# First loads side by side, and the first weights' high part in halves, in a hybrid retention and attention layer

## The chip, the cores and the metric

The kernel runs on one core of one Trainium2 chip. The metric is the device time of one execution in microseconds (us), of which the median over several runs is taken. A core has TensorE (PE in the profile; PEld are its weight loads, which overlap its matmuls), VectorE (DVE), ScalarE (ACT), GpSimd (POOL) and SyncE (SP), which here only issues DMAs. ACT can issue DMAs too, on a queue of its own.

## The reference

One decoder layer on x of 1 x 2048 x 1024 in float32. The input is normalised, one projection makes all parts, two groups of heads run side by side, and a projection back is added to x.

```python
h = rms_norm(x, norm_w)
proj = einsum('bsd,de->bse', h, w_in)          # 1024 -> 2816
rq, rk, rv, rg, sq, sk, sv, sg = split(proj)
ro = retention(rotary(rq), rotary(rk), rv)     # 4 heads, chunks of 128, decaying state
ro = group_norm(ro) * ret_norm_w * silu(rg)
so = sliding_window_attention(sq, sk, sv, ...) # 8 heads, window 128, sinks, bias
so = so * silu(sg)
x = x + einsum('bse,ed->bsd', concat([ro, so]), w_out)
```

## The kernel before

**Products.** The two projections are four big products over the 2048 rows (2048 x 1024 by columns of `w_in` from 768, from 0 and from 1792, then by `w_out`). Each is done with seven block products instead of eight (a Strassen scheme), for pairs of 128-row chunks. `weights` (L528) makes the seven combinations of a weight's four quarters, `blocks` (L583) those of x. Each operand is held as a high part in the matmul's reduced format (fp32r) and a low part that holds the rest; a block product is, for each of four blocks k of 128 rows of the weights, three matmuls: high x by high w, high x by low w, low x by high w (`passes` in `products`, L662). `split` (L479) makes the two parts: ACT copies the raw tile to the high part, scaled by a column of norm_w (`nw_sb`) where it is a raw weight, and DVE makes raw minus high.

**The opening.** The first four products of the first projection run together. `opening` (L630) loads, for each of four blocks k, the columns of x that they need (`xfirst[k]`, 128 x 512) and splits them in two halves of 256 columns; `products` runs for k < 3 all four high by high matmuls, then all four by the low w, then all four with the low x, so that the parts are needed one after the other (L692 to L698). The very first product matmul needs the first half of the high x of k = 0 and the high w of k = 0.

**Ahead of it.** The last part of `layer` (from L1370) loads `nw_sb` from ACT's queue (cost `BESIDE`, L411), makes a zero tile `none`, runs WARM matmuls on it (`warm`, L1376 to L1380; each shows as two in the profile) and one ACT instruction (`once`) that brings in ACT's table.

**The order of work.** Every instruction is an operation with a cost per engine, the tiles that it reads and writes, and a due time. `Program.emit` (L158) is a planner that runs when the kernel is built: it keeps a clock for every engine and for the DMA queue (Q, which is SP), and always takes the operation that can start first, the one due sooner where they tie; this gives the order in which each engine gets its instructions. An operation with several engines in its cost goes to the one that can start it first. `load` (L413) goes to Q unless a cost is given. All operations pass through one helper, so that nearly every instruction has line L362 in the profile, and tiles tell them apart: `acc` are the banks of the products, `w` and `x` the operands' tiles, `m` the other matmuls' banks.

Of the kernel before, what the change touches and what calls it, by code (L numbers as in the profile page):

```python
# [30 lines left out]
F32R = mybir.dt.float32r  # L31
I32 = mybir.dt.int32
AF = mybir.ActivationFunctionType
ALU = mybir.AluOpType
# [3 lines left out]
S, D = 2048, 1024  # L38
P = 128
NCH = S // P  # L40
NP = NCH // 2
KT = D // P
# [37 lines left out]
OPENING = 4  # L80
SEM = 0.06

WARM = 4

BACKLOG = 1.5

# [37 lines left out]
class Program:  # L124
# [5 lines left out]
    def op(self, cost, go, r=(), w=(), due=0.0, table=None, label="", also=()):  # L130

        o = Op()
        o.cost, o.go, o.due, o.after, o.set, o.label = cost, go, due, [], table, label
        o.n, o.left, o.ready, o.end, o.seen, o.by = len(self.ops), 0, 0.0, 0.0, 0.0, None
        deps = set()
        for b in r:
            if b.writer is not None:
                deps.add(b.writer)
        for b in w:
            if b.writer is not None:  # L140
                deps.add(b.writer)
            deps.update(b.readers)
        for b in r:
            b.readers.append(o)
        for b in w:
            b.writer, b.readers = o, []
        o.bufs = list(dict.fromkeys((*r, *w, *also)))
        for b in o.bufs:
            b.left += 1
        o.new = [b for b in (*w, *also) if b.ap is None and b.tag]  # L150
        for d in deps:
            if d is not o:
                d.after.append(o)
                o.left += 1
        self.ops.append(o)
        return o
# [142 lines left out]
def dve(n, two=False, lat=0.08):  # L299
    return (0.067 + n / 960, 0.067 + n / 960 + lat, two)  # L300


def act(n, more=0.0):
    return (0.094 + n / 1200 + more, 0.2 + n / 1200 + more, False)
# [6 lines left out]
def both(n):  # L311
    return {"V": dve(n, True)}
# [21 lines left out]
def dma(kb, issue=0.45):  # L334
    return {"Q": (0.45 + kb / 1024, 2.6, issue)}
# [27 lines left out]


@with_exitstack
def layer(ctx, tc, xt, xfirst, xtok, nw, w_in, w_rn, qkw, sinks, biasg, rope, dmask, gpow, w_out, out):
    nc = tc.nc
    order = Order(tc)
    V, G, A, Q, T = (Engine(order, e) for e in (nc.vector, nc.gpsimd, nc.scalar, nc.sync, nc.tensor))
# [16 lines left out]
    op = prog.op  # L386

    def kb(name, share, dtype=F32):
        return Buf("k", None, dtype, name, share)
# [10 lines left out]
    def fixed(shape, name, dtype=F32):  # L400
        return Buf(name=name, ap=const.tile(shape, dtype, name=name))
# [5 lines left out]
    def given(ap):  # L407
        return Buf(ap=ap)


    BESIDE = {"A": (0.4, 3.5, False)}  # L411

    def load(b, src, due, kbytes=256, to=lambda t: t, cost=None, also=(), of=lambda t: t):  # L413
        op(
            cost or dma(kbytes), lambda e: e.dma_start(to(b()), of(src())), [src], [b], due, label=f"load {b.name}",
            also=also,
        )
# [4 lines left out]
    def f(t):  # L422
        return t.bitcast(F32)

    ident = fixed([P, P], "ident")
    nw_sb = fixed([P, KT], "nw_sb")
    wr = fixed([P, 4], "wr")
    gp = fixed([P, 2], "gp")
    snk = fixed([P, AH], "snk")
# [98 lines left out]
    def weights(src, c0, n, scale, base, seq):  # L528


        W = {m: [None] * 4 for m in range(1, 8)}
        at = {m: base + seq.first[m] for m in W}
        col, cols = scale

        def raw(q, i, due):
            t = kb("w", "wr")
            k, c = 4 * (q // 2) + i, c0 + q % 2 * n
            load(
                t, given(src[k * P : (k + 1) * P, c : c + n]), due - 3, n // 2, lambda t: t[:, :n],
            )  # L540
            return t

        def by(k):
            return (col, k) if k < cols else None

        def part(m, i, t, scale=None):
            W[m][i] = split(t, n, at[m] - 1.5 + 0.1 * i, "wh", "w", scale)

        b11, b21, t1, t2 = ([None] * 4 for _ in range(4))
        for i in range(4):  # L550
            due = at[1] - 2 + 0.1 * i
            t = b11[i] = raw(0, i, due)
            part(1, i, t, by(i))
        for i in range(4):
            b21[i] = raw(2, i, at[2] - (2 if base else 0.9) + 0.1 * i)
            part(2, i, b21[i], by(4 + i))
        for i in range(4):
            t = b11[i]
            op(
                {"A": act(n, 0.09), "V": (0.13 + n / 1920, 0.2 + n / 1920, True)},  # L560
                lambda e, t=t, i=i: e.activation(t()[:, :n], t()[:, :n], AF.Copy, scale=col()[:, i : i + 1])
                if e is A
                else e.tensor_scalar(t()[:, :n], t()[:, :n], col()[:, i : i + 1], None, op0=ALU.mult),
                [t, col, W[1 if base else 2][3][1]], [t], at[1] + 2 + i, label="scale w",
            )
        for i in range(4):
            due = at[6] - 6 + 0.5 * i
            b12, b22 = raw(1, i, due), raw(3, i, due)
            t1[i] = combine(b12, b11[i], ALU.subtract, n, due, b12, scale=by(i))
            t2[i] = combine(b22, t1[i], ALU.subtract, n, due, b22, scale=by(4 + i))  # L570
            part(6, i, t2[i])
        for i in range(4):
            part(5, i, t1[i])
        for i in range(4):
            due = at[7] - 4 + 0.5 * i
            part(7, i, combine(t2[i], b11[i], ALU.subtract, n, due, b11[i]))
            part(4, i, combine(b21[i], t2[i], ALU.subtract, n, due, b21[i], scale=by(4 + i)))
        for i in range(4):
            part(3, i, raw(3, i, at[3] - 2 + 0.1 * i), by(4 + i))
        return W  # L580
# [49 lines left out]
    def opening():  # L630

        made = []
        for k in range(KT // 2):
            t, hi, lo = kb("x", "raw"), kb("x", "x", F32R), kb("x", "x", F32R)

            load(t, given(xfirst[k]), -4.95 + 0.1 * k)
            parts = []
            for i in range(2):
                c, due = slice(i * 256, (i + 1) * 256), -2.0 + 0.1 * k + 0.01 * i
                h, l = (Part(t, lambda t, c=c: t[:, c]) for t in (hi, lo))  # L640
                op(
                    {"A": act(256), "V": dve(256)} if k == 0 else {"A": act(256)},
                    lambda e, t=t, h=h, c=c: e.activation(h(), t()[:, c], AF.Copy) if e is A else e.tensor_copy(h(), t()[:, c]),
                    [t], [h], due, label="hi x", also=(hi, lo),
                )
                op(
                    both(256), lambda e, t=t, h=h, l=l, c=c: e.tensor_tensor(l(), t()[:, c], f(h()), ALU.subtract),
                    [t, h], [l], due, label="lo x", also=(hi, lo),
                )
                parts.append((h, l))  # L650
            made.append((hi, lo, parts))
        return made
# [4 lines left out]
    def products(B, W, n, base, seq, sink, plus=None, opening=None):  # L657


        s, u, t, bank = {}, {}, {}, {}  # L660

        def passes(m, acc, xh, xl, cols, k, d, goes_on, parts, which):  # L662


            wh, wl = W[m][k]

            def go(e):
                for i in which:
                    a, b = ((xh, wh), (xh, wl), (xl, wh))[i]
                    e.matmul(  # L670
                        acc()[:, :n], a()[:, cols], b()[:, :n], start=(not goes_on and k == i == 0),
                        stop=(k == 3 and i == 2), skip_group_check=goes_on,
                    )

            pairs = ((parts[0], wh), (parts[0], wl), (parts[1], wh))
            reads = list(dict.fromkeys(b for i in which for b in pairs[i]))
            op(f32r(n, len(which)), go, reads, [acc, turn], d, label=f"product {m}", also=(xh, xl, wh, wl))

        for m, p in seq.all:
# [12 lines left out]
            elif p == OPENING - 1:  # L692
                for k, (xh, xl, parts) in enumerate(opening):

                    for which in ((0,), (1,), (2,)) if k < 3 else ((0, 1, 2),):
                        for q in range(OPENING):
                            due = (OPENING * k + q) / 4
# [670 lines left out]


    make_identity(nc, ident())  # L1370
    load(nw_sb, given(nw), -9, 4, cost=BESIDE)

    pw, none = ps(), kb("none", "att")
    op({"V": (0.2, 0.3, False)}, lambda e: e.memset(none()[:, 0:256], 0.0), [], [none], -9, label="nothing")
# [1 line left out]
    def go(e):  # L1376
        for _ in range(WARM):
            e.matmul(pw()[:, 0:256], none()[:, 0:P], none()[:, 0:256], start=True, stop=True)

    op({"T": (0.85 * WARM, 0.85 * WARM + 0.2, False)}, go, [none], [pw], -9, label="warm")  # L1380

# [5 lines left out]
        label="no values",  # L1387
# [34 lines left out]


_SHAPES = {
    "xt": (NCH, P, KT * P), "xfirst": (KT // 2, P, OPENING * P), "xtok": (NCH, P, D), "nw": (P, KT), "w_in": (D, 2816), "w_rn": (P, 4),
    "qkw": (P, 2, HD), "sinks": (P, AH), "biasg": (P, 2, GRP, 320), "rope": (NCH, P, 2, 256),
    "dmask": (P, RH, P), "gpow": (P, 2), "w_out": (D, D),
}
# [89 lines left out]
```

## Time and profile before

| | |
|---|---|
| median of three runs | 717.34 us (717.23 to 718.02) |
| the profiled execution | 717.6 us |
| its span, first to last instruction | 715.3 us |
| PE busy | 710.6 us (99%) |
| DVE, ACT busy | 603.5 us (84%), 437.1 us (61%) |
| first product's weight load | 4.71 us |
| HBM read, written | 110.44 MB, 42.01 MB |

The times inside the span are counted from its first instruction. A row of a view names the engine, the operation, the tiles (written <- read), the shapes and the number of instructions; the bracket at the end tells how long the engine was idle before and what ended that. A row with a q behind the engine's name is an issue of a DMA, and its duration is that of the issue, not of the transfer. Matmul records are pipelined: one lasts longer than the step to the next.

### The profile page before, as it was taken

What the parts mean: (1) busy time and instruction counts of PE and PEld (TensorE: products, weight loads), DVE (VectorE), ACT (ScalarE), POOL (GpSimd) and SP (SyncE); (2) the same over time, 40 slices, a digit from 0 to 9 for tenths busy, and PEclk for the clock granted to TensorE, in tenths of its full rate; (3) what the DMA queues carried; (4) which work ended last, traced back from release to release, by engine and by line L of the source; (5) the groups of instructions that cost most, each with busy time, mean ns of one, the idle gap of its engine ahead of it and who ended that gap; (6) DMA issues with size and microseconds to landing.
All of it is one profiled execution on the core that took longest, in us unless ns stands there. A gap on an engine that the chain in (4) does not pass through costs nothing.

```text
span 715.3 us, 15310 instructions
## 1 busy us (share of the span) xinstructions
PE 710.6 (99%) x5388; PEld 608.9 (85%) x5388; DVE 603.5 (84%) x1456; ACT 437.1 (61%) x1071; POOL 43.6 (6%) x75
## 2 busy tenths in 40 slices
PE   9999999999999999999999999999999999999998
PEld 7888888889999999988888888888888888888886
DVE  6999877876999777899899899878999998677762
ACT  8565966657776465787687875686875437321500
POOL 1000000025111000001000001000000000000000
PEclk9999999999999999999999999999999999999999
DMA  9978948966657268979896585199391422223722
GB/s 329 360 250 309 399 133 305 306 233 219 223 160 222 75 204 255 331 240 320 278 318 192 148 282 159 47 360 371 112 325 52 148 88 75 89 88 119 264 97 95
DMA packets 102028, 153.46 MB, mean 215 GB/s; under 512 B 11840, under 2 KB 40512, under 8 KB 101952
## 3 DMA queue, kind: packets, MB, share of 16 engines
q1 hardware_dynamic: 101808, 152.49, 63.5%
q8 instruction: 42, 0.69, 0.4%
q14 instruction: 34, 0.28, 0.1%
q10 hardware_dynamic: 144, 0.00, 0.0%
HBM read 110.44 MB, written 42.01 MB: 213 GB/s over the span
## 4 chain that ended last, share of the span: by engine, by line
PE 99%; DVE 0%; issue 0%
PE acc L362 81%; PE m L362 18%; DVE t L362 0%; DVE none L362 0%
## 5 line engine op out<-in xcount | busy, mean ns | idle before, releaser
L362 PE MATMUL acc<-w,x 128*128 128x512 f32 (+1 forms) x2700 | 604.4, 379 | 0.0
L362 PEld LDWEIGHTS acc<-w,x 128*128 128x128 f32 x2700 | 489.0, 188 | 79.6 <-issue 4.3
L362 DVE TENSOR_TENSOR x<-x 128x512 fp32r<-128x512 f32 (+2 forms) x220 | 145.1, 680 | 17.7 <-ACT x L362 16.5
L362 ACT ACTIVATE x<-x 128x512 fp32r<-128x512 f32 (+1 forms) x187 | 111.4, 617 | 13.6 <-PE acc L362 10.0
L362 ACT ACTIVATE pm<-lg,nm 128x128 f32<-128x128 f32 x128 | 49.8, 391 | 29.3 <-DVE lg L362 28.0
L362 DVE TENSOR_TENSOR w<-w 128x512 fp32r<-128x512 f32 (+3 forms) x96 | 61.6, 666 | 6.2 <-ACT w L362 6.0
L362 DVE TENSOR_TENSOR s<-acc,s 128x512 f32<-128x512 f32 (+1 forms) x64 | 41.8, 654 | 21.3 <-PE acc L362 20.9
L362 ACT ACTIVATE w<-w 128x512 fp32r<-128x512 f32 (+1 forms) x72 | 40.5, 600 | 26.4 <-DMA w<-in_w_out 18.4
L362 DVE SCALAR_TENSOR_TENSOR w<-w,nw_sb 128x512 fp32r<-128x512 f32 (+3 forms) x72 | 49.9, 709 | 0.7 <-ACT w L362 0.7
L362 DVE CUSTOM_DVE_ANT_0 lg<-m,bias,nsnk 128x160 f32<-128x160 f32 x128 | 42.5, 378 | 4.5 <-PE m L362 4.3
L362 POOL TENSOR_SCALAR_AFFINE_SELECT own<-pT 64x512 f32<-64x512 f32 x32 | 27.4, 868 | 257.3 <-ACT pT L362 227.0
L362 ACT ACTIVATE x<-go 128x512 fp32r<-128x512 f32 x40 | 23.8, 623 | 24.2 <-PE acc L362 21.0
L362 DVE TENSOR_TENSOR t<-acc,t 128x512 f32<-128x512 f32 (+2 forms) x33 | 21.0, 636 | 16.4 <-PE acc L362 16.2
L362 ACT ACTIVATE s<-acc 128x512 f32<-128x512 f32 (+1 forms) x32 | 17.9, 567 | 26.0 <-PE acc L362 20.1
L362 DVE TENSOR_TENSOR t<-acc,s 128x512 f32<-128x512 f32 (+1 forms) x32 | 21.0, 655 | 10.9 <-PE acc L362 10.7
L362 ACT ACTIVATE w<-w,nw_sb 128x512 fp32r<-128x512 f32 (+3 forms) x43 | 27.9, 682 | 3.0 <-DMA w<-in_w_in 1.9
L362 DVE TENSOR_TENSOR r<-acc,t 128x512 f32<-128x512 f32 (+1 forms) x32 | 20.9, 653 | 8.6 <-PE acc L362 7.7
L362 DVE TENSOR_TENSOR x<-go,x 128x512 fp32r<-128x512 f32 x40 | 27.1, 681 | 0.0
L362 ACT ACTIVATE ro<-ro,nmu,rg 128x128 f32<-128x128 f32 x64 | 25.1, 483 | 0.1
L362 ACT ACTIVATION_READ_ACCUMULATOR pm<-lg,nm 128x1 f32 x128 | 24.1, 189 | 0.0
L362 ACT ACTIVATE xk<-xk 128x512 f32<-128x512 f32 x32 | 19.8, 619 | 6.3 <-DMA xk<-in_xtok 6.3
L362 ACT ACTIVATE pT<-m 128x512 f32<-128x512 f32 x32 | 18.6, 595 | 5.9 <-PE m L362 5.6
(132 smaller groups left out, 695.4 us busy)
## 6 DMA issues: line engine op xcount, KB each, us to landing
x<-in_xt SPq DMA_DIRECT2D x80, 256.0 KB, 5.1
x<-s_dram SPq DMA_DIRECT2D x64, 256.0 KB, 4.1
w<-in_w_in SPq DMA_DIRECT2D x40, 256.0 KB, 5.4
s_dram<-x SPq DMA_DIRECT2D x32, 256.0 KB, 4.9
xk<-in_xtok SPq DMA_DIRECT2D x32, 256.0 KB, 5.1
res<-in_xtok SPq DMA_DIRECT2D x32, 256.0 KB, 3.2
w<-in_w_out SPq DMA_DIRECT2D x20, 256.0 KB, 4.5
aq<-aq_dram SPq DMA_DIRECT2D x16, 256.0 KB, 4.4
```

Source lines behind the costliest of these rows:

```text
L362: return lambda *a, **k: self.order.put(op(*a, **k))
```

## The change

The scale of the rows, norm_w, no longer has a load of its own. On the host it is put beside the first block of `xfirst` in one array (`xnw`, 128 x 520); one load from SP brings both into a fixed tile `x_nw`, of which `first_x` and `nw_sb` are parts. The load of the first raw weight tile goes to ACT's queue instead. The high part of that weight is made in two halves of 256 columns, the first on ACT, the second on DVE (`first_split`); the low part comes as before in one DVE instruction. Of the first x, the first half's high part is fixed to DVE and the second's to ACT, with other due times. WARM goes from 4 to 3. A product that reads high w of k = 0 now names both halves.

```diff
-WARM = 4
+WARM = 3
...
-    BESIDE = {"A": (0.4, 3.5, False)}
+    BESIDE = {"A": (0.4, 3.3, False)}
...
-    nw_sb = fixed([P, KT], "nw_sb")
+    x_nw = fixed([P, OPENING * P + KT], "x_nw")
+    first_x = Part(x_nw, lambda t: t[:, : OPENING * P])
+    nw_sb = Part(x_nw, lambda t: t[:, OPENING * P :])
...
+        def first_split(raw, n, due):
+            hi, lo = kb("w", "wh", F32R), kb("w", "wh", F32R)
+            parts = [Part(hi, lambda t, i=i: t[:, i * n // 2 : (i + 1) * n // 2]) for i in range(2)]
+            for i, part in enumerate(parts):
+                def go(e, i=i, part=part):
+                    src = raw()[:, i * n // 2 : (i + 1) * n // 2]
+                    if i == 0:
+                        e.activation(part(), src, AF.Copy, scale=col()[:, 0:1])
+                    else:
+                        e.tensor_scalar(part(), src, col()[:, 0:1], None, op0=ALU.mult)
+                cost = {"A": act(n // 2, 0.09)} if i == 0 else {"V": (0.13 + n / 1920, 0.2 + n / 1920, True)}
+                op(cost, go, [raw, col], [part], due, label="hi w", also=(hi, lo))
+            op(
+                {"V": (0.13 + n / 960, 0.21 + n / 960, True)},
+                lambda e: e.scalar_tensor_tensor(
+                    lo()[:, :n], raw()[:, :n], col()[:, 0:1], f(hi()[:, :n]), op0=ALU.mult, op1=ALU.subtract
+                ),
+                [raw, *parts, col], [lo], due - 2, label="lo w", also=(hi,),
+            )
+            return hi, lo, parts
...
                 t, given(src[k * P : (k + 1) * P, c : c + n]), due - 3, n // 2, lambda t: t[:, :n],
+                BESIDE if base == q == i == 0 else None,
...
-            part(1, i, t, by(i))
+            if base == i == 0:
+                W[1][0] = first_split(t, n, due + 0.5)
+            else:
+                part(1, i, t, by(i))
...
-            t, hi, lo = kb("x", "raw"), kb("x", "x", F32R), kb("x", "x", F32R)
-            load(t, given(xfirst[k]), -4.95 + 0.1 * k)
+            t = kb("x", "raw") if k else first_x
+            hi, lo = kb("x", "x", F32R), kb("x", "x", F32R)
+            if k:
+                load(t, given(xfirst[k - 1]), -4.95 + 0.1 * k)
...
+                if k == 0:
+                    due -= 1.0
...
-                    {"A": act(256), "V": dve(256)} if k == 0 else {"A": act(256)},
+                    ({"V": dve(256)}, {"A": act(256)})[i] if k == 0 else {"A": act(256)},
...
-                    [t], [h], due, label="hi x", also=(hi, lo),
+                    [t], [h], due + (1.6 if k == 0 and i else 0), label="hi x", also=(hi, lo),
...
-            wh, wl = W[m][k]
+            wh, wl, *halves = W[m][k]
+            whole = halves[0] if halves else (wh,)
...
-            pairs = ((parts[0], wh), (parts[0], wl), (parts[1], wh))
+            pairs = ((parts[0], *whole), (parts[0], wl), (parts[1], *whole))
...
-    load(nw_sb, given(nw), -9, 4, cost=BESIDE)
+    op(dma(258), lambda e: e.dma_start(x_nw(), xnw), [], [first_x, nw_sb], -9, label="load x")
```

More of the change, by code (lines that the diff above doesn't have):

```diff
@@ L365, in layer @@
 @with_exitstack
-def layer(ctx, tc, xt, xfirst, xtok, nw, w_in, w_rn, qkw, sinks, biasg, rope, dmask, gpow, w_out, out):
+def layer(ctx, tc, xt, xfirst, xtok, xnw, w_in, w_rn, qkw, sinks, biasg, rope, dmask, gpow, w_out, out):
     nc = tc.nc
@@ L1424 @@
 _SHAPES = {
-    "xt": (NCH, P, KT * P), "xfirst": (KT // 2, P, OPENING * P), "xtok": (NCH, P, D), "nw": (P, KT), "w_in": (D, 2816), "w_rn": (P, 4),
+    "xt": (NCH, P, KT * P), "xfirst": (KT // 2 - 1, P, OPENING * P), "xtok": (NCH, P, D), "xnw": (P, OPENING * P + KT), "w_in": (D, 2816), "w_rn": (P, 4),
     "qkw": (P, 2, HD), "sinks": (P, AH), "biasg": (P, 2, GRP, 320), "rope": (NCH, P, 2, 256),
@@ L1490 @@
     x2 = x.reshape(NCH, P, KT, P)
+    first = x2[: 2 * OPENING : 2, :, : KT // 2].transpose(2, 3, 0, 1).reshape(KT // 2, P, OPENING * P)
     given = {
         "xt": x2.transpose(0, 3, 2, 1).reshape(NCH, P, KT * P),
-        "xfirst": x2[: 2 * OPENING : 2, :, : KT // 2].transpose(2, 3, 0, 1).reshape(KT // 2, P, OPENING * P),
+        "xfirst": first[1:],
         "xtok": x.reshape(NCH, P, D),
-        "nw": norm_w.reshape(KT, P).T,
+        "xnw": np.concatenate([first[0], norm_w.reshape(KT, P).T], axis=1),
         "w_in": w_in[:, _columns()],
```

## The prediction

> **What bounds the kernel now.** I read the first and fourth parts of the page, then three stretches of the span, then the chain's first pieces.
>
> ```profile
> PE 710.6 (99%) x5388; PEld 608.9 (85%) x5388; DVE 603.5 (84%) x1456; ACT 437.1 (61%) x1071; POOL 43.6 (6%) x75
> ...
> PE 99%; DVE 0%; issue 0%
> ```
>
> ```profile
> 5.00:155.00 150.00, 150.00 (x666) 124.18 (x665) 129.28 (x238) 102.26 (x230) 5.29 (x16) 1.00 0.85 295
> 155.00:563.00 408.00, 408.00 (x4050) 358.29 (x4049) 362.03 (x1039) 288.89 (x760) 35.42 (x48) 1.00 0.68 223
> ```
>
> ```profile
> 1.26 3.78 PE m L362 x8
> 5.04 149.67 PE acc L362 x660
> ```
>
> PE is busy for the whole of both stretches (second and third figures of each row equal) and for 710.6 of 715.3 us in all. The 4.7 us without PE work are the 1.26 before the warming matmuls and the end (3.4), which the change does not touch. So no product waits for anything once the products run; a product matmul comes every 149.67/660 = 0.227 us. Time can be won or lost in three ways only: by when the first product starts, by the rate of the first products, and by the order that the planner writes for the rest. The first of these is to be read in the timeline of the opening, in order of time per engine, with the time from issue to landing of the first transfers (last column of the five lines of the second fence, each from the stretch of its own issue: w, nw, x, the second w, the second x).
>
> ```profile
> 0.81 0.41 ACTq L362 DMA_DIRECT2D nw_sb<-in_nw  x1
> ...
> 0.81 0.39 SPq L362 DMA_DIRECT2D w<-in_w_in  x1
> ...
> 1.25 0.42 SPq L362 DMA_DIRECT2D x<-in_xfirst  x1
> ...
> 1.73 0.42 SPq L362 DMA_DIRECT2D w<-in_w_in  x1
> ...
> 3.87 0.72 ACT L362 ACTIVATE w<-w,nw_sb 128x512 fp32r<-128x512 f32 x1 [1.12 <-DMA nw_sb<-in_nw]
> ...
> 4.30 0.29 DVE L362 CAST x<-x 128x256 fp32r<-128x256 f32 x1 [3.10 <-DMA x<-in_xfirst]
> 4.49 0.40 ACT L362 ACTIVATE x<-x 128x256 fp32r<-128x256 f32 x1
> ...
> 4.62 0.75 DVE L362 SCALAR_TENSOR_TENSOR w<-w,nw_sb 128x512 fp32r<-128x512 f32 x1
> 4.71 11.30 PEld L362 LDWEIGHTS acc<-w,x 128*128 128x128 f32 x50 [0.40 <-ACT w L362]
> ...
> 5.29 0.76 DVE L362 TENSOR_TENSOR x<-x 128x256 fp32r<-128x256 f32 x2
> 5.96 0.72 ACT L362 ACTIVATE w<-w,nw_sb 128x512 fp32r<-128x512 f32 x1 [1.07 <-DMA w<-in_w_in]
> 6.64 0.73 ACT L362 ACTIVATE x<-x 128x256 fp32r<-128x256 f32 x2
> ```
>
> ```profile
> w<-in_w_in SPq DMA_DIRECT2D x1, 256.0 KB, 2.8
> nw_sb<-in_nw ACTq DMA_DIRECT2D x1, 4.0 KB, 3.0
> x<-in_xfirst SPq DMA_DIRECT2D x1, 256.0 KB, 3.0
> w<-in_w_in SPq DMA_DIRECT2D x1, 256.0 KB, 4.2
> x<-in_xfirst SPq DMA_DIRECT2D x1, 256.0 KB, 4.4
> ```
>
> The first w is there at 0.81 + 2.8 = 3.6, the row scales nw at 3.8, the first x at 1.25 + 3.0 = 4.3. ACT makes the high part of w from 3.87 to 4.59; DVE makes the first half of the high x from 4.30 to 4.59. Two chains end together, and PE's first weight load starts 0.12 later, at 4.71.
>
> **The change part by part.**
>
> **Loads.** The load of nw goes; its 4 KB travel as eight columns more of the first x (258 KB in place of 256). That load becomes SP's first, at 0.81 instead of 1.25; the first w goes to ACT's queue at 0.81, in nw's place, so ACT's own work (table load, `once`) does not move. SP's later loads each go out one place, about 0.48 us, sooner (the second w at 1.25 in place of 1.73). Side by side in this way is not in the trace, so it is bounded. At best each lands 2.8 after its issue, as the first w did: both at 3.6. At worst, as the same 512 KB move through the same DMA engines, the later of the two lands when the second did before: 4.3. Nw, which ran beside w on the other queue, took 3.0 with its 4 KB, more than w with 256 KB, so the queues do share the engines; I take the middle, T = 3.95, and keep 3.6 to 4.3.
>
> [...]
>
> **High parts.** Before, w's high part was ready to be made when x was still on its way; now neither half can start before T, since nw comes with x. DVE does the high x first (an earlier due time, both ready at once), then the second half of the high w. The price of that half (256 columns, scaled) is not in the trace; the nearest rows are the CAST above (0.29) and DVE's scaling of 512 columns:
>
> ```profile
> L362 DVE TENSOR_SCALAR w<-w,nw_sb x3: 476/476/478, 14.0 to 15.4; 128x512 f32<-128x512 f32 x3
> ```
>
> Bounds 0.24 (half of it) and 0.48; I take 0.31, near the CAST. ACT's half, with 0.40 for 256 columns of x and (0.72 in the rows above for 512 scaled) at most 0.5, ends before DVE's pair. First product: T + 0.02 (landing to CAST, as 4.28 to 4.30) + 0.29 + 0.02 + 0.31 + 0.12 = T + 0.76. For T = 3.6 / 3.95 / 4.3 that is 4.36 / 4.71 / 5.06, against 4.71 now: 0.35 earlier, nothing, 0.35 later. The earlier x and the longer work behind it pay for each other.
>
> **Behind it, on DVE and ACT.** By the planner's rule (earliest start first) DVE's order becomes high x, high w half, low x half, low w, low x half. The high half ends 0.12 before the first product starts (the hop to PE); then come a low half (0.34: half of the step from 5.29 to the pair's end at 6.05, less their overlap) and the low w (0.75), and the hop again: ready 0.34 + 0.75 = 1.1 after the first product's start. It is needed after four matmuls, 4 x 0.227 = 0.9 at full rate and 1.1 with the first at the slow rate of the fences below: its cover (now 5.37 + 0.12 = 5.5, needed at 5.8) is gone, and 0 to 0.2 us of wait follow; I take 0.05. The second half of the high x moves on ACT from 4.49 to about T + 0.5 = 4.45 and is needed two matmuls in: hidden. The second block of rows starts after twelve matmuls, near 4.71 + 12 x 0.227 + 0.2 = 7.6; its high x is ready at 6.64 + 0.42, so 0.4 to 0.5 us of cover remain even if the first product is 0.35 earlier and the loads land no sooner. So no stall follows there; if the loads do land sooner, the cover only grows. No wait is added that has other work queued behind it on ACT: before T it has only the table load and `once`.
>
> **Warming.** One warming matmul of four goes. How it is paid is seen in PE's own groups (duration minimum/median/maximum; the warming weight loads and matmuls, then product matmuls before 5.2, then from 5.4):
>
> ```profile
> L362 PEld LDWEIGHTS m<-none x8: 287/337/337, 1.3 to 4.0; 128*128 128x128 f32 x8
> L362 PE MATMUL m<-none x8: 634/634/794, 1.3 to 4.4; 128*128 128x256 f32 x8
> ```
>
> ```profile
> L362 PE MATMUL acc<-w,x x2: 390/468/546, 4.7 to 5.1; 128*128 128x512 f32 x2
> ```
>
> ```profile
> L362 PE MATMUL acc<-w,x x38: 387/389/397, 5.4 to 13.8; 128*128 128x512 f32 x38
> L362 PEld LDWEIGHTS acc<-w,x x37: 187/188/188, 5.6 to 13.8; 128*128 128x128 f32 x37
> ```
>
> A weight load takes 337 ns in the warming and 188 in the products, the first product matmul 546 and all later ones 389: PE's clock rises to full at about 4.9 us, 3.6 us after PE's first work at 1.26, in the midst of the first product. The page's granted clock reads 1.00 throughout and does not show that step. The eight warming instructions (two for each matmul) start every (4.4 - 1.3)/7 = 0.44 us, so six have passed by 1.26 + 6 x 0.44 = 3.9 in place of 4.8 for eight. The matmul that goes therefore reached to where products start now; kept, it would hold up a product that came sooner. Between 3.9 and 4.7 PE would now stand idle for 0.8 us. My choice: the clock still rises near 4.9, as over three quarters of the time before it are busy. Then an earlier start counts only half (matmuls before 4.9 run at half rate), a later one fully.
>
> **The planner.** Its own clock sees the first product about 0.3 us sooner and the loads one place sooner, and the order of the rest can shift. Every order that keeps PE fed gives the same sum of matmuls; what differs is how often PE changes between products and the small matmuls. The nearest row is the weight loader's idle time at such changes:
>
> ```profile
> PEld m L362 <- issue: 9.1, 44, 0.4
> ```
>
> About 0.2 us each; I cost the new order at nothing, with bounds of three changes fewer or more, -0.6 and +0.6.
>
> **Sum.** Against the profiled execution, 717.6 with 2.3 around its span of 715.3: start 0 (-0.2 to +0.35), low w +0.05 (0 to +0.2), order 0 (-0.6 to +0.6): 717.6 + 0.05. That run lies 0.26 above the median of the three, 717.34, so the forecast is 717.4, its own range 716.6 to 718.3.
>
> **The rivals.**
>
> **The clock rises later (slower).** With one warming matmul fewer the work before 4.7 is 2.6 us and then there is a hole of 0.8. If the rise needs unbroken work of the length seen now (1.26 to 4.9, 3.6 us), the count starts again at the first product and the rise comes at 4.71 + 3.6 = 8.3. All product matmuls from 4.71 to 8.3 then run at half rate; now it is only those to 4.9. Cost (3.6 - 0.2)/2 = 1.7 us: 719.1, 0.24% slower. It decides from the point where 2.6 us of work and a pause of 0.8 are too little for the rise. For it: the rise comes so soon after the fourth warming matmul's end. Against: nothing shows that a shorter stretch or one with a hole would not do. Chance 0.28.
>
> [...]
>
> **The planner's order (either way).** From 7 of the 44 changes, 1.4 us, it crosses the line: 715.9 or 718.8, or a transfer placed late leaves PE waiting, which nothing does now. For it: DVE at 129 of 150 us and DMA at 0.85 in the first stretch leave little room there. Against: PE is never short in 707 us, and a uniform shift changes no comparison in the planner. Slower 0.08, faster 0.12, the latter because the forecast has no other road to a large gain.
>
> **Side by side works at its best.** Both land at 3.6, products from 4.36: half of 0.35, 0.2 us gained, 717.2. It lies inside the forecast. **The change does nothing:** both interleave fully (T = 4.3) and the start comes 0.35 later: 717.7, inside it too.
>
> **How the numbers follow.** A measurement of this kernel can tell about 0.2%, 1.4 us, from no change. Forecast with the two cases inside it 0.52 (within), clock 0.28 and order 0.08 (slower), order 0.12 (faster). Faster 0.12, same 0.52, slower 0.36. For 8 in 10 the range reaches over the clock's 719.1 plus 0.2, and below to 716.4, where most of the faster order is left out: 716.4 to 719.3.
>
> **What would show it.** Right: the first product between 4.4 and 5.1; the two first loads landing between 3.6 and 4.3; on DVE the CAST, then a 256-column scaling of about 0.3; product matmuls of 389 ns from about 4.9 on; PE full between 5 and 563. The clock rival: product matmuls well above 389 ns to about 8.3. The order rival: PE idle, or more or fewer changes, behind 155. Wrong outright: a first product before 4.3, or a PE wait at the second block of rows near 7.6.

## The result, and the profile after

The changed kernel takes 719.62 us (median of 22 runs, 717.49 to 720.29), the kernel before 717.38 (22 runs, 716.93 to 718.53). The ratio of the runs is 1.0023, with a 95% interval of 1.0016 to 1.0031: slower, by an interval that leaves out no change. (It is the ratio of the means, 719.26 and 717.59, and not that of the two medians, 1.0031: the changed kernel's runs form two groups, six from 717.49 to 717.88 and sixteen from 719.24 to 720.29 with nothing between, and the median lies in the upper one.) The median, 719.62, lies 0.3 above the range predicted (716.4 to 719.3); by the ratio the change makes 719.0 of the 717.34 that the forecast started from, which lies inside. Either way it is outside the likeliest case's own range: it is the rival of the late clock that came true, with another loss added that I had bounded too low.

The time around the span, from 1.7 to 3.0 us in all these runs, differs from run to run, so spans are compared from here on. Before (its spans in the runs beside the experiments): 715.1 to 716.7, median 715.8 in 32 runs and 715.9 in 35 others. Changed: six from 715.8 to 716.1, sixteen from 717.5 to 718.5.

The profile of the change happens to be of the lower group (717.88, span 716.1). Its page, engines' busy time and chain:

```profile
PE 710.0 (99%) x5386; PEld 608.5 (85%) x5386; DVE 603.7 (84%) x1456; ACT 437.4 (61%) x1072; POOL 42.2 (6%) x75
...
PE 99%; DMA 1%; ACT 0%; DVE 0%; issue 0%; ACTq 0%
```

PE's busy time is the same within 0.6. A DMA has come into the chain, which before was PE alone from the warming on (all but DVE's zero tile ahead of it). The chain's first pieces in order of time (start, duration) show which:

```profile
0.81 4.29 DMA w<-in_w_in
5.74 150.62 PE acc L362 x663
```

The first w, now on ACT's queue, takes 4.29 us to land, and products start at 5.74, where they started at 4.7. The transfers issued first, with their time to landing in the last column:

```profile
x_nw<-in_xnw SPq DMA_DIRECT2D x1, 260.0 KB, 4.1
w<-in_w_in ACTq DMA_DIRECT2D x1, 256.0 KB, 4.3
```

Before, x took 3.0 and w 2.8. The timeline of the opening, from the first warming matmul on:

```profile
1.26 2.93 PE L362 MATMUL m<-none 128*128 128x256 f32 x6 [1.26 <-DVE none L362]
...
4.93 0.30 DVE L362 CAST x<-x_nw 128x256 fp32r<-128x256 f32 x1 [3.73 <-DMA x_nw<-in_xnw]
5.14 0.35 DVE L362 TENSOR_SCALAR w<-w,x_nw 128x256 fp32r<-128x256 f32 x1
5.18 0.51 ACT L362 ACTIVATE w<-w,x_nw 128x256 fp32r<-128x256 f32 x1 [2.44 <-DMA w<-in_w_in]
...
5.74 0.75 DVE L362 SCALAR_TENSOR_TENSOR w<-w,x_nw 128x512 fp32r<-128x512 f32 x1
5.74 10.34 PEld L362 LDWEIGHTS acc<-w,x 128*128 128x128 f32 x46 [2.28 <-ACT w L362]
5.74 10.54 PE L362 MATMUL acc<-w,x 128*128 128x512 f32 x45 [1.56 <-ACT w L362]
```

Nw lands with x at 4.91 and w at 5.09. DVE's two instructions behind x end at 5.49, ACT's half of w at 5.69, and that one releases PE. PE is without work from 3.98, when the sixth warming instruction has passed (it starts at 3.56, and they come every 0.427 us), to 5.74: this is the hole.

Here is the changed kernel's other group, from a second profile of it (span 717.8), beside the first. The product matmuls from 5.2 to 9.0, duration minimum/median/maximum in ns, of the first and then of the second profile:

```profile
L362 PE MATMUL acc<-w,x x14: 387/395/505, 5.7 to 8.9; 128*128 128x512 f32 x14
```

```profile
L362 PE MATMUL acc<-w,x x8: 628/628/797, 5.4 to 8.6; 128*128 128x512 f32 x8
```

The same instructions, in the same order, take 395 ns in the one and 628 in the other. In the second they start every 0.427 us until 9.5, then every 0.227. The trace's own record of the granted clock, whose first entry is the rise to full, has it at 4.49 in the first profile and at 9.55 in the second (the clock's column of the stretches reads 1.00 ahead of that entry too, and tells nothing there). In the kernel before it is at 4.91. So the upper group is the late clock.

Nothing else moved. The middle of the span in the changed kernel, where PE is busy throughout as in the row of the kernel before that the prediction shows:

```profile
155.00:563.00 408.00, 408.00 (x4050) 358.58 (x4050) 361.38 (x1038) 288.75 (x760) 34.06 (x48) 1.00 0.68 223
```

From the first product to the span's end it is 710.53 us before, 710.39 in the first profile (clock up already) and 712.31 in the second. Ahead of the rise a share of 0.200/0.427 = 0.47 of the time is lost, by the two steps above: 0.08 of the 4.91 - 4.75 before, and 1.92 of the 9.55 - 5.45 in the second profile. Without it the three are 710.45, 710.39 and 710.39. The planner's new order costs nothing that these profiles show.

### The profile page after: what moved, and what is told of

The parts are those of the page before. It is cut to its first block, busy times and chain, and to the rows that moved or that the text cites. A ratio compares the mean times of both kernels' runs of the same rounds, so it can differ in the third digit from the quotient of the medians.

```text
span 716.1 us, 15324 instructions
## 1 busy us (share of the span) xinstructions
PE 710.0 (99%) x5386; PEld 608.5 (85%) x5386; DVE 603.7 (84%) x1456; ACT 437.4 (61%) x1072; POOL 42.2 (6%) x75
## 4 chain that ended last, share of the span: by engine, by line
PE 99%; DMA 1%; ACT 0%; DVE 0%; issue 0%; ACTq 0%
PE acc L362 81%; PE m L362 18%; DMA w<-in_w_in 1%; ACT w L362 0%; DVE t L362 0%; ACTq L362 0%
## 5 line engine op out<-in xcount | busy, mean ns | idle before, releaser
L362 DVE SCALAR_TENSOR_TENSOR w<-w,x_nw 128x512 fp32r<-128x512 f32 (+3 forms) x72 | 50.3, 712 | 0.1
L362 ACT ACTIVATE w<-w,x_nw 128x512 fp32r<-128x512 f32 (+4 forms) x44 | 28.1, 675 | 3.9 <-DMA w<-in_w_in 3.9
L362 DVE TENSOR_REDUCE hs<-sq 128x8 f32<-128x512 f32 (+1 forms) x32 | 15.5, 485 | 8.8 <-ACT sq L362 8.4
```

What stands on the lines that cost most here:

```text
L362: return lambda *a, **k: self.order.put(op(*a, **k))
```

## The experiments

**The changed kernel once more**, for a profile of its upper group (the one shown above).

> The changed kernel as it is, for a second profile of it. Clock theory: in about three quarters of its runs the grid has no stretch with enough work ahead of the first product; then the span is 717.5 to 718.5, product matmuls come every 0.427 us from the first product (5.3 to 5.8) until the clock rises between 8.1 and 10.8, and every 0.227 us from there. In the other quarter the span is 715.8 to 716.1 and they come every 0.227 us from the start. Rival (a stall behind the first product or another order makes the slower group): matmuls every 0.227 us from the start, and the missing 2 us as PE idle time elsewhere.

Measured: span 717.8, first product at 5.45, steps of 0.427 us to the rise at 9.55. As expected, and PE is full from 155 to 712 us, as in the first profile.

**More warming in the changed kernel.**

```diff
-WARM = 3
+WARM = 5
```

> The changed kernel with five warming matmuls in place of three, nothing else. Clock theory: the warming fills the hole ahead of the first product (it ends near 1.26 + 5 x 0.85 = 5.5, the first product comes at 5.74), so the runs near 719.2 to 720.3 vanish: all of them between 717.2 and 718.8, median about 717.9, 1.7 below the change. Rival (the later first product and another order make the loss, the clock has no part): median stays at 719.6, in two groups as before.

```profile
1.26 4.63 PE L362 MATMUL m<-none 128*128 128x256 f32 x10 [1.26 <-DVE none L362]
5.36 2.81 PEld L362 LDWEIGHTS acc<-w,x 128*128 128x128 f32 x11 [0.19 <-ACT w L362]
```

These are rows of its timeline up to 8.0. The idle time of the weight loader ahead of the products is 0.19 in place of 2.28. The tenth warming instruction passes at 5.69 and holds the first product up: the second product matmul follows it 0.76 behind, 0.33 more than the 0.427 of a step ahead of the rise. Measured: 717.83 (717.60 to 718.88), spans 715.7 to 716.5 in all eleven runs; the upper group is gone. Ratio to before 1.0004 (0.9995 to 1.0012). The first product is still late, at 5.36, yet most of the loss has gone: the upper group comes from the hole.

**Four in place of three.**

```diff
-WARM = 3
+WARM = 4
```

> The changed kernel with four warming matmuls in place of three. Warming ends near 4.8, first product at 5.4 to 5.7, so the hole is 0.6 to 0.9 and a stretch that holds it all has 0.73 to 0.83 of PE's work. Clock theory: most runs rise early (717.5 to 718.8), a few late (over 719.2), median near 718.0. Rival (the later first product alone): 719.6 in two groups, as with three.

Measured: seven spans from 715.8 to 716.4, four from 717.8 to 718.4, median time 718.09, ratio 1.0009 (0.9999 to 1.0019). Between the two others, as a hole of half the length (4.83 to 5.63 in its profile) should be: with three warming matmuls 16 of 22 runs were late, with four 4 of 11, with five none of 11.

**The hole alone, in the kernel before.** Loads, halves and order stay as they were before.

```diff
-WARM = 4
+WARM = 2
```

> The kernel before with two warming matmuls in place of four, loads as they were. Clock theory: a hole from 3.0 to 4.7 in PE's work makes the clock rise late in most runs: first product still near 4.7, median about 719 (717.3 in the few early ones, up to 720 in the late ones). Rival (warming does not matter, the loads make the loss): 717.4 as before, spread 716.9 to 718.5.

```profile
1.26 2.08 PE L362 MATMUL m<-none 128*128 128x256 f32 x4 [1.26 <-DVE none L362]
4.82 3.53 PE L362 MATMUL acc<-w,x 128*128 128x512 f32 x8 [1.49 <-DVE x L362]
```

In this timeline the first product comes as before, at 4.82, but only eight matmuls start up to 8.0 (in the kernel before fourteen: 4.75 + 0.385 for the first + 12 x 0.23 = 7.9). Measured: 719.00 (718.43 to 719.66), ratio 1.0016 (1.0008 to 1.0025); spans 716.7 to 717.9, the rise at 7.96 in the profile. The hole by itself makes the kernel slower. That a few runs would rise early was wrong: none of the eleven spans is as short as the early ones of the kernel before. Two warming matmuls hold 3.13 - 1.26 = 1.87 us of work, too little by the bound that the next experiment gives.

**The step of the change alone, in the kernel before.**

```diff
-WARM = 4
+WARM = 3
```

> The kernel before with three warming matmuls in place of four, nothing else. Theory now: the clock rises at the end of the first 3.41 us stretch of a fixed grid in which PE worked for about three quarters; 2.5 of 3.41 (0.74, first run with one queue) were too little, 2.7 (0.80, the change's profile) enough. Here a stretch with the whole hole (4.0 to 4.75) has 2.65 of 3.41, 0.77, between the two: either spans stay at 715.2 to 716.7 as before (the threshold is below 0.77), or about two thirds of them go to 717 to 718 (it is above). Rival (the loads alone make the loss): spans as before, first product at 4.75 in both.

Measured: 718.23, spans 715.1 to 715.7 in seven runs, 716.4 in one and 717.2 to 717.8 in four; ratio 1.0009 (0.9999 to 1.0020). Neither branch of the expectation whole: it is the borderline itself, a third of the runs late. In its profile (span 716.4) the rise came at 7.34; one stretch of the grid sooner, at 3.92, PE had worked for 3.92 - 1.26 = 2.66 us, and that was not enough. In the change's first profile the stretch up to 4.49 held 3.98 - 1.26 = 2.72, and that was. (How the grid is read from the traces is told in the part on why the prediction was right or wrong.)

**One queue.** The first w goes back to SP's queue, ahead of x with nw.

```diff
-                BESIDE if base == q == i == 0 else None,
...
-    op(dma(258), lambda e: e.dma_start(x_nw(), xnw), [], [first_x, nw_sb], -9, label="load x")
+    op(dma(258), lambda e: e.dma_start(x_nw(), xnw), [], [first_x, nw_sb], -4.95, label="load x")
```

> The changed kernel with the first w back on SP's queue ahead of the load of x and nw, everything else (rows of 2080 bytes, halves, three warming matmuls) as changed. Theory A (two queues side by side slow the first transfers): w lands near 3.7 and x with nw near 4.3, first product near 5.0. Theory B (the rows of 520 columns do it): x with nw lands at 4.8 or later, first product at 5.5 or later. Time in either: still two groups, since the hole in PE's work remains (3.9 to 5.0 or to 5.5); median 718.5 to 719.5.

```profile
x_nw<-in_xnw SPq DMA_DIRECT2D x1, 260.0 KB, 2.9
w<-in_w_in SPq DMA_DIRECT2D x1, 256.0 KB, 2.7
```

```profile
4.85 3.06 PEld L362 LDWEIGHTS acc<-w,x 128*128 128x128 f32 x8 [1.38 <-ACT w L362]
```

Issued one behind the other, at 0.81 and 1.25, w lands at 3.5 in place of 5.09 and x at 4.2 in place of 4.91, and the first product comes at 4.88 in place of 5.74. That speaks for theory A: the second queue delays both. The rows of 520 columns cost nothing here (2.9 to landing; rows of 512 took 3.0 in the kernel before). The hole from 4.0 to 4.9 stays, and so do two groups: three spans from 715.4 to 715.6, eight from 717.1 to 718.4; 719.07, ratio 1.0010 (1.0000 to 1.0020).

**Side by side, but rows of 512 columns.** X comes from `xfirst` as before, first on SP's queue, nw by a load of its own behind it; the arrays given change with it.

```diff
-    op(dma(258), lambda e: e.dma_start(x_nw(), xnw), [], [first_x, nw_sb], -9, label="load x")
+    load(first_x, given(xfirst[0]), -9)
+    load(nw_sb, given(nw), -8.9, 4)
...
```

> The changed kernel with x in rows of 512 columns again, first on SP's queue, and nw by a load of its own behind it; w beside them on ACT's queue as changed. Theory A (two queues side by side): w and x still land near 4.9 to 5.1, first product near 5.7. Theory B (rows of 520 columns): w and x land by 4.3, nw at about 4.3 (1.25 + 3.0), first product near 5.0. Time: two groups in both, median 719 to 719.6 by A, 718.5 to 719.5 by B.

```profile
x_nw<-in_xfirst SPq DMA_DIRECT2D x1, 256.0 KB, 3.5
w<-in_w_in ACTq DMA_DIRECT2D x1, 256.0 KB, 3.7
x_nw<-in_nw SPq DMA_DIRECT2D x1, 4.0 KB, 3.5
```

Both are slower than on one queue also with the old rows: x at 4.35, w at 4.55, nw at 4.73. Median 719.81, ratio 1.0020 (1.0008 to 1.0033), three of nine runs in the lower group. The landings lie between the two theories, nearer to B's 4.3 than to A's 4.9 to 5.1, and the first product, at 5.38, midway. Two more profiles of the same kernel followed.

> The kernel with w and x side by side in rows of 512 columns and nw by its own load, a second look. In four looks at loads as changed the later of the pair landed at 4.7 to 5.1; the first look here gave 4.55. If the row of 520 columns costs something beside the second queue, the later of the pair lands below 4.7 again; if not, somewhere from 4.5 to 5.1.

> The same kernel, a third look: below 4.7 again if the row of 520 columns costs something beside the second queue, from 4.5 to 5.1 if not.

Measured: w at 4.56 and 4.69, x at 4.36 and 4.51 (one run each, 717.77 and 717.98, spans 715.9 and 716.0: both of the lower group). In all three profiles w, the later of the pair, lands from 4.55 to 4.69; in the four with the joined rows (the change twice, with four and with five warming matmuls) at 5.09, 4.80, 4.99 and 4.71. So the second queue itself adds 0.2 to 0.6 (4.12 to 4.36 for the later of the pair in six profiles with one queue for both). The joined rows' profiles lie 0 to 0.5 above that, and why stays open: by the edit it can be the rows, but also what SP issues next, at 1.25, which is the second w of 256 KB with them and the 4 KB of nw here.

The packets of the transfers tell the three cases apart too. From 2 to 3 us 112 to 146 of them pass with one queue (six profiles, nw's own packets of 32 bytes left aside), 92 to 104 with two queues and the old rows (three), 66 to 86 with two queues and the joined rows (four). In the change's first profile the 80 are 44 of x and 36 of w: neither transfer has that time to itself, and fewer packets pass in all.

**Both suspects undone**, the rest of the change kept: one queue as above, and

```diff
-WARM = 3
+WARM = 4
```

> The changed kernel with both suspects undone: first w back on SP's queue ahead of x with nw, and four warming matmuls; the halves, the joined array and the due times stay. Theory (the shared transfers and the hole make the whole loss): first product near 4.9, no run in a late group, spans 715.3 to 716.8 and median within 0.3 of the kernel before. Rival (the halves on DVE or the new order cost too): more than 0.5 above the kernel before.

```profile
4.82 0.76 PEld L362 LDWEIGHTS acc<-w,x 128*128 128x128 f32 x4 [0.50 <-ACT w L362]
...
5.75 2.38 PEld L362 LDWEIGHTS acc<-w,x 128*128 128x128 f32 x11 [0.18 <-DVE w L362]
```

Measured: 717.45 (716.92 to 718.87), spans 715.2 to 716.4 with a median of 715.7, ratio 0.9999 (0.9990 to 1.0007): the kernel before again. The two suspects make the whole loss. They act together: the runs with only one of them come to 1.0009 (the change with four warming matmuls), 1.0009 (the kernel before with three) and 1.0010 (one queue), with intervals that reach to no change, and both make 1.0023. The second row is the wait for the low w after four matmuls that the prediction's order led to: 0.18 for the weight loader, and nothing for the matmuls, which go on every 0.23 to 0.24 us over it.

**The halves alone**, in the kernel before: `first_split` for the first w, loads, due times of x and warming as before.

> The kernel before with only the high part of the first weights in two halves on ACT and DVE; loads, dues of x and four warming matmuls as before. Theory: w is ready about 0.3 sooner, but x lands at 4.3 as before, so the first product stays at 4.7 to 4.8; spans and median as before (within 0.3). Rival (the halves by themselves matter): first product 0.2 or more away from 4.75.

```profile
4.74 2.66 PEld L362 LDWEIGHTS acc<-w,x 128*128 128x128 f32 x12 [0.42 <-ACT x L362]
```

W is no longer the releaser; the high part of x, which lands at 4.3, is. First product at 4.77; 718.14 (716.94 to 718.95), spans 715.1 to 716.9 with a median of 715.6, ratio 1.0007 (0.9998 to 1.0015). No change can be told: the high x was ready no sooner than the high w before (both at 4.6).

No version here beats the kernel before.

## Why the prediction was right or wrong

Of the signs that the prediction named, the 256-column scaling on DVE (0.35) and, in the lower group, matmuls at about 390 ns came; the first product (5.45 and 5.74, not 4.4 to 5.1) and the landings (4.60 to 5.09, not 3.6 to 4.3) did not. That the ratio comes as near the rival's 719.1 as 719.0 is in part luck: two losses were added, and six runs of 22 escaped the larger. The likeliest case's own range also holds a slip: by its own bounds it ends at 717.34 + 0.35 + 0.2 + 0.6 = 718.5, not 718.3, and the 258 KB of the joined load are 260. Neither changes the account.

**The loads: the worst case was not one.** The step that failed is "At worst, as the same 512 KB move through the same DMA engines, the later of the two lands when the second did before: 4.3." It took shared engines, read from nw's 3.0 us for 4 KB beside w's 2.8 for 256 KB, to mean the same end for the same bytes. On two queues the later one landed at 4.55 to 5.09 in all seven profiles, on one queue at 4.12 to 4.36. T was sized 3.95; x was there at 4.35 to 4.91 and w 0.2 later. X was issued 0.44 sooner (0.81 in place of 1.25) and landed 0.07 to 0.63 later than the 4.28 before: the second queue lost time. Both transfers were under way together (44 packets of x and 36 of w from 2 to 3 us in the change's first profile). Why fewer packets pass from 2 to 3 us with two queues, 66 to 104 in place of 112 to 146, no run here shows.

**The high parts.** T + 0.76 was the sum; with T as x's landing it measured 5.74 - 4.91 = 0.83. DVE's half took 0.35, not 0.31, but DVE was not last: w landed 0.18 after x, and ACT's half (0.51, bounded at 0.5) released PE. Small misses. With one queue x landed at 4.12 and 4.16, up to 0.16 sooner than the 4.28 before, and the first product came at 4.85 and 4.88, 0.1 later than 4.75: the longer work behind x cost a little more than the sooner landing gave.

**The wait for the low w** was put at 0 to 0.2. There was none in the changed kernel (DVE ends it at 6.49, and four matmuls from 5.74 on need until 6.79), and with one queue and four warming matmuls the 0.18 was the weight loader's alone. At the second block of rows the prediction looked at the high x only. The changed kernel's first profile has no wait there; with one queue and four warming matmuls its low w came late, the weight loader stood idle for 0.28 ahead of 8.65, and the two matmuls around it took 0.13 longer than the usual step.

**The warming: my choice failed.** "the clock still rises near 4.9, as over three quarters of the time before it are busy" took a moment of one run for fixed, and set the point too low. The clock's record gives the rise and the fall at the end of each run. Between them lie 709.97 us in ten of the thirteen traces, 713.39 in two and 706.56 in one: three values 3.41 apart, which fit one grid of 3.413 us for both (208, 209 and 207 steps of it). How full a stretch of the grid has to be, the runs bound: of the stretches that ended without a rise the busiest held 2.66 us of PE's work, of those that ended with one the least busy held 2.72 (four traces); by these runs the point is 0.78 to 0.80 of 3.413, if PE's work is counted from the first instruction's start to the last one's next step. The grid's place differs from run to run: with four warming matmuls and a first product at 4.75 to 4.85, the rise came at 4.34, 4.87 and 4.91. With 2.69, the middle of the two, as the point, three warming matmuls (1.26 to 3.98) make only a stretch that ends between about 1.26 + 2.69 = 3.95 and 3.98 + 3.41 - 2.69 = 4.70 busy enough: 0.75 of 3.41, 22% of the runs if every place of the grid is as likely, an estimate; 6 of 22 did it. All others would have to wait for a stretch filled by products, as the second profile did to 9.55. With four and a first product at 4.75 every place of the grid would by the same estimate give a rise by 1.26 + 2.69 + 3.41 = 7.36. A rise that late would cost (7.36 - 4.75) x 0.47 = 1.2 us, an estimate, which would also explain most of the spread of the kernel before, 715.1 to 716.7; no profile of it with a late rise is on record.

**The sizes.** In the lower group the change loses what the first product is late, 715.8 to 716.1 against 715.1 to 715.2 for the early runs of before. The upper group, 717.5 to 718.5, is 1.4 to 2.7 longer, of which the clock was 1.92 in the one profile; the rival had 1.7, for a first product at 4.7 with one rise a whole 3.6 us behind it. The half rate in its sum was a step of 0.427 against 0.227 us in the second profile, 0.53 of the full rate. My rival said "the count starts again at the first product"; the runs do not fit a count that starts again, as the rise came 2.66 us behind the first product in one (4.68 to 7.34, the kernel before with three warming matmuls) and 4.10 in another (5.45 to 9.55, the second profile), where 3.6 was expected. They fit a stretch of a grid that has to be full enough, which in the second profile cost about as much. What I gave a chance of 0.28 is what came: the late loads made the hole 1.5 to 1.8 us long where I had 0.8. With the first product where I put it (the kernel before with three warming matmuls, at 4.7), 4 of 12 runs were clearly late, and its median was not; that 4 of 12 is near 0.28 means nothing, as the 0.28 was for the kernel's median and not for single runs.

**The planner's order** moved much (the products and small matmuls behind 155 us come in other groups), and not the time: within 0.1 us from first product to end, the slow clock taken off.

## What to carry to other kernels

Warming matmuls are not judged by whether one ends where the real work starts, but by the hole that they leave. In these runs the clock rose at the end of a 3.413 us stretch in which PE was busy for 2.72 us or more, and not after 2.66 or less, and the stretches fell differently from run to run: fill up to the latest start that the loads can have. One matmul too many held the first product up by 0.33 us here; a hole of 0.7 us made 4 of 12 runs some 2 us longer. A second DMA queue for two transfers that are both awaited can end both later than one queue in order: here they landed at 4.35 to 4.91 and 4.55 to 5.09 on two, at about 3.5 to 3.7 and 4.12 to 4.36 on one. When the runs of one kernel fall into two groups, a profile of one group does not explain the other: here the first one was of the rarer group and did not show the larger part of the loss.

## What the runs showed that I had not expected

Two transfers of 256 KB issued at the same time on two queues landed 3.5 to 4.3 us after issue, the same two one behind the other on one queue 2.7 to 3.1 after theirs. The clock did not rise after stretches of 3.413 us with up to 2.66 us (0.78) of PE's work, and rose after ones with 2.72 (0.80) or more. The place of the grid against the kernel's start is not fixed (rises at 4.34, 4.87 and 4.91 with the same warming): by the estimate above, that alone can move the span of the kernel before, unchanged, by 1.2 us.
